# Attention probabilities turned in 32x32 blocks on VectorE and over DRAM instead of on TensorE

## The chip, the cores and the metric

The kernel runs on one core of a Trainium2 chip. The metric is device time in microseconds (us): the median of the runs of one program. A profile is one execution; its span runs from the first to the last instruction. The engines are called by their short names: PE is TensorE (matmuls, and the transposes made with a matmul by the identity), DVE is VectorE, ACT is ScalarE, POOL is GpSimd, and SP is the engine that issues nearly all DMAs.

## The reference

One layer of an encoder over 512 tokens of width 1024, in float32. After an RMSNorm, one projection gives the columns of two branches: attention (8 query heads of 128 in 2 groups, one key and value head each) and a gated delta rule (8 heads, forward and backward). Both are merged through sigmoid gates, projected, added to x after a norm, and a gated per-layer embedding is added. The part that changes is attention:

```
def block(qi):                       # 128 queries at a time
    s = einsum('bkgqd,bksd->bkgqs', qi, k) * scale
    pr = softmax(s, axis=-1)
    return einsum('bkgqs,bksd->bkgqd', pr, v)
...
y_att = (o_att * silu(az)) @ w_br_att
```

`az` is the gate of the attention branch, a projection of the same normed input.

## The kernel before, in words

Every float32 matmul of the large projections is split: each operand is kept as a rounded high part (fp32r) and a low part, and three matmuls (low by high, high by low, high by high) are summed. ACT writes the high part, and DVE or POOL subtracts it to get the low one (`split`). One matmul moves 512 columns; a weight slab (128 output columns, all 1024 inputs) takes 24 of them.

The order of the work is made at build time by a planner (`Flow`). Each piece of the kernel is a Python generator that asks for buffers (`yield "get", tag`), moments (`"at"`), events (`"ev"`) and PE time (`"pe"`); `A`, `V`, `G`, `W` and `Q` put an operation on ACT, DVE, POOL, DVE with POOL kept away, or the DMA queue of SP, each with a length by a table of costs written into the code. The planner runs the generators against these lengths, and the moments that come out fix the order of the instructions on each engine; on the chip each engine works in that order. The text `ORDER` lists the PE jobs: projections (`dk`, `dq`, `dv` of the delta rule, the gates `az`, `dz`, `gA`, `gB`, `kv`, `q0`, `q1`), then the branch projections `ydn` and `yatt`, the output projection `out0`, `out1` and the embedding gate `pg0`, `pg1`. `PR` holds priorities, `OUT0` the places of the four weight blocks of `out0` in the loads, `COOL` and `HOT` the bias between DVE and POOL for a split of data in SBUF, and `SPARE` the large buffers that are lent to the weight stream for a while.

Large buffers are the units `u0` to `u16` (128 partitions of 8 KB). `c2` (four buffers of 128x512), `blk` (three pairs of 128x512), `gi` and `go` (two each, gates in and out), `whi`, `wlo` and `wraw` (two each, weights) and the PSUM banks `mm` (five) and `aux` (three) are the small ones.

Attention before: `q_job` projects four heads at once (`q0`, `q1`), `q_tail` norms and rotates them, and `q_done` starts all eight heads once both halves are ready. In `att_head(h)` PE makes a 128x512 tile of scores for each of four query tiles; DVE takes the row maximum, ACT the exponential with the row sum; DVE inverts the sum and POOL multiplies the tile by it. Then for each of four key tiles PE transposes four 128x128 squares into a bank `mm` by the identity, ACT and DVE split that into `blk`, and three matmuls add to the output `po` (`pv`). The gate `az`, kept in DRAM since its projection, multiplies `po`, and the split result goes to `ya`, the input of `yatt`.

The delta rule already has another way to transpose: `small_blocks` turns each 32x32 block on DVE, and `turned` writes the blocks to DRAM and reads them back to their places.

Of the kernel before, what the change touches and what calls it, by code (L numbers as in the profile page):

```python
# [17 lines left out]
NT = 4  # L18
# [17 lines left out]
class Flow:  # L36
# [73 lines left out]
    def ready(self, want):  # L110
        kind = want[0]
        if kind == "at":
            return want[1]
        if kind == "ev":
            return want[1].t
        s = self.slots[want[1]]
        return min(s) if s else None

# [5 lines left out]
    def run(self):  # L124
        while self.parts:
            best, soon = None, None
            for p in self.parts:
                r = self.ready(p[3])
                if r is None:
                    continue  # L130
                if r <= self.now + 1e-9:
                    if best is None or p[:2] < best[:2]:
                        best = p
                elif soon is None or r < soon:
                    soon = r
            if best is None:
                if soon is None:
                    raise RuntimeError("stuck: " + ", ".join(f"{p[0]} {p[2].__name__} {p[3][:2]}" for p in self.parts))
                self.now = soon
                continue  # L140
            if best[3][0] == "get":
                s = self.slots[best[3][1]]
                s.remove(min(s))
            self.flush()
# [12 lines left out]


ORDER = """
dk0 vec dk1 dq0 dq1 dq3 dq2 dk2 az4 dk3 dv1 dv3 dq5 dv0 dq7 dz7  # L160
dk5 dv2 az3 dz5 dz3 az6 gB2 gB4 dz0 az0 gA3 dk4 dk7 dz4 dq6 dq4
gA4 dk6 gA6 gB5 dz1 dz2 dv7 dv4 dv5 gA0 az1 gA5 gB0 gA2 dv6 az2
gA1 kv gA7 gB7 az7 gB6 gB3 q0 gB1 dz6 q1 az5 free_h ydn0 ydn6 ydn7
ydn5 ydn3 ydn1 ydn2 ydn4 yatt1 yatt0 yatt5 yatt3 yatt7 yatt2 yatt6 yatt4 out0 out1 pg0
# [6 lines left out]
SPARE = ((15, "raw", 7.0, 190.0), (11, "pair", 22.0, 80.0), (12, "pair", 22.0, 80.0), (14, "pair", 279.0, 375.0),  # L171
         (13, "pair", 443.0, 525.0))
EOUT = 24.0
WIDE = 2.0
LAND = "c2"
LONG, NEAR = 0.6, 1.5
X_DVE = ()
WARM = 5.5
W1 = 0
COOL, HOT = 2.5, -1.5  # L180


@with_exitstack
def layer(ctx, tc, x, xT, pw0, wp1, wt, wba, wn, rows, qkn, hd16, npost, pnorm, dnorm, cs, out):
# [261 lines left out]


    slab, blocks, fetched = {}, {}, {}

    lent = {"raw": {}, "pair": {}}  # L450
    held = {}
# [43 lines left out]
    def loader(names):  # L495
        for name in names:
            yield "ev", fetched[name]
            raw, t = load[name]
            if name[:2] in places:
                us, j = places[name[:2]], name[2]  # L500
                his, los = blocks.setdefault(name[1], ([], []))
                if j % 2 == 0:
                    for u, lst in ((us[j // 2], his), (us[j // 2 + 2], los)):
                        yield "get", f"u{u}"
# [979 lines left out]
    def q_job(b, qus):  # L1484
# [5 lines left out]
        o = yield from gemm_k(f"q{b}", hh, hl)  # L1490
        for t in range(NT):
            att_ev[b, t] = spawn(q_tail(b, t, o[t]), PR["q"])
        if b == 1:
            spawn(q_done(), 4)

    def q_done():
        for b in range(2):
            yield "ev", stat_ev["q", b]
            for t in range(NT):
                yield "ev", att_ev[b, t]  # L1500
        free("u16")
        for h in range(8):
            head_ev[h] = spawn(att_head(h), PR["head"] + 0.01 * h)
        att_start.set(F.now)

    head_ev = {}
    att_start = Event()
    ya = [None, None]

    def att_head(h):  # L1510
        hb, kv, b = h % 4, h // 4, h // 4
        qh, ql = qbs[b]
        akT, av = akv["k"], akv["v"]
        if h % 2 == 0:
            yield "get", "u16"
            pu = unit(16, [128, 4, 512])
            P = [pu[:, t, :] for t in range(NT)]
        else:
            P = []
            for t in range(NT):  # L1520
                yield "get", "c2"
                P.append(tile("c2", [128, 512]))
        uz, tz = yield from gate_in("az", h)
        tp = []
        for t in range(NT):
            cc = slice(t * 128, (t + 1) * 128)
            yield "get", "aux"
            sc = bank("aux")
            pe.matmul(sc, ql[:, hb, cc], akT[:, 0, kv, :], start=True, stop=False)  # L1529
# [21 lines left out]
            free("blk", F.now + 0.7)  # L1551

        pend = []
        for kt in range(NT):
            yield "get", "mm"
            pt = bank("mm")
            for t in range(NT):
                pe.transpose(pt[:, t * 128:(t + 1) * 128], P[t][:, kt * 128:(kt + 1) * 128], ident)  # L1558
            yield "pe", 0.436
            yield "get", "blk"  # L1560
            pT = tile("blk", [128, 2, 512], F32R)
            _, tl = split(pt, pT[:, 0], pT[:, 1], F.now, 512)
            free("mm", tl)
            pend.append((kt, pT, tl))
            if len(pend) > 1:
# [4 lines left out]
        if h % 2 == 0:  # L1570
            free("u16")
        else:
            for t in range(NT):
                free("c2")
        k_, p_, t_ = pend.pop(0)
        yield "at", t_ + 0.3
        pv(k_, p_)
        yield "pe", 0.682
# [77 lines left out]
    def yatt_job(n):  # L1656
# [7 lines left out]
        o = yield from gemm_t(("yatt", n), sel(ya, 0), sel(ya, 1), [head_ev[h] for h in range(8)])  # L1664
        att_ev["mix", n] = spawn(yatt_tail(n, o, pre), 5)
        if turn("yatt") == 7:
            for u in (13, 14, 9, 10):
                free(f"u{u}")


# [67 lines left out]
    def out_job(half, us):  # L1738
# [1 line left out]
            yield "get", "u12"  # L1740
            late["mx0"] = unit(12, [128, 4, 512])
        else:
            for u, lst in zip((0, 1, 2, 3), (x1Th, x1Th, x1Tl, x1Tl)):
# [151 lines left out]
    def job(kind, n=0):  # L1895
        if kind in ("dk", "dq", "dv"):
            return conv_job, kind, n
        if kind in GATES:
            return gate_job, kind, n
        return {"kv": (kv_job,), "q": (q_job, n, ((9, 10), (11, 12))[n % 2]), "ydn": (ydn_job, n), "yatt": (yatt_job, n),  # L1900
                "out": (out_job, n, ((0, 1, 2, 3), (6, 15, 16, 11))[n % 2]), "free_h": (call, free_h),
                "vec": (call, late_vectors), "pg": (pg_job, n, ((13, 14, 9, 10), (6, 15, 16, 11))[n % 2])}[kind]
# [93 lines left out]
```

## Time and profile before

| what | value |
|---|---|
| runs | 750.6, 752.1, 752.03 us; median 752.03 |
| span of the profiled execution | 749.9 us |
| what lies around it in the median | 2.1 us |
| PE, DVE, ACT, POOL busy | 98%, 63%, 47%, 42% of the span |
| bytes moved by DMA | 110.99 MB, 148 GB/s in the mean |
| attention on PE (scores to last probability matmul) | 516.3 to 609.9 us (first and last start) |

A row of the profile names the line, the engine, the operation and the tiles it writes and reads (with buffer numbers left out, so `u` is any large unit). Line L122 is the planner's call of an operation, L102 the same for long POOL operations and L97 for those that keep POOL away, so those rows are told apart by their tiles. The profile gives an execution's span and not its whole time; it is set beside the median.

### The profile page before, as it was taken

To read this page: it belongs to the slowest core of one execution; us is meant where nothing else is said; L and a number is where in the kernel's file an instruction comes from. 1 tells how busy PE (TensorE), PEld (TensorE's weight loads), DVE (VectorE), ACT (ScalarE), POOL (GpSimd) and SP (SyncE) were. 2 spreads that over 40 slices of the span, in tenths; PEclk is the share of its full clock that TensorE was granted. 3 is DMA by queue.
4 is the path that set the end of the run, shared out by engine and by line. 5 is a ranking of instruction groups with operands and counts; after the bars stand their busy time and mean duration, and the time that the engine had idled before them with its cause. 6 is when DMAs were issued, how large, how long until landed. Compare 5 with 4: busy or idle time off the path is not lost.

```text
span 749.9 us, 11919 instructions
## 1 busy us (share of the span) xinstructions
PE 736.5 (98%) x4441; PEld 617.5 (82%) x4441; DVE 473.6 (63%) x924; ACT 353.2 (47%) x668; POOL 315.1 (42%) x284
## 2 busy tenths in 40 slices
PE   9999999999899999999999999999999999999996
PEld 7688888888688898888789988888888888888885
DVE  4688989887875657997384535438667744314434
ACT  6659474544552265442633245334576633332422
POOL 5836585213233265300531155657446434561501
PEclk9999999999999999999999999999999999999999
DMA  8854456687402244756521134435233446552323
GB/s 347 299 199 129 162 173 186 197 271 233 116 30 71 76 156 114 229 175 199 138 73 43 43 113 140 154 111 200 87 97 115 137 167 213 176 180 94 99 66 117
DMA packets 65994, 110.99 MB, mean 148 GB/s; under 512 B 22353, under 2 KB 31505, under 8 KB 65937
## 3 DMA queue, kind: packets, MB, share of 16 engines
q1 hardware_dynamic: 65648, 109.98, 45.2%
q8 instruction: 35, 0.57, 0.3%
q10 hardware_dynamic: 288, 0.26, 0.1%
q14 instruction: 23, 0.18, 0.1%
HBM read 87.11 MB, written 23.10 MB: 147 GB/s over the span
## 4 chain that ended last, share of the span: by engine, by line
PE 94%; DMA 2%; ACT 1%; DVE 1%; issue 0%; POOL 0%; POOLq 0%; DVEq 0%
PE mm L534 17%; PE mm L536 17%; PE mm L535 17%; PE mm L555 4%; PE mm L553 4%; PE mm L554 4%; PE mm L571 3%; PE mm L572 3%; PE mm L573 3%; PE aux L1203 2%; PE aux L1235 2%; PE mm L1558 2%; PE aux L1221 2%; PE aux L1194 1%; PE aux L1183 1%; PE aux L1529 1%
## 5 line engine op out<-in xcount | busy, mean ns | idle before, releaser
L102 POOL TENSOR_TENSOR wlo<-wraw,whi 128x1024 fp32r<-128x1024 f32 x52 | 124.3, 2393 | 208.1 <-ACT whi L122 205.4
L534 PE MATMUL mm<-u,wlo 128*128 128x512 f32 x504 | 203.6, 404 | 2.6 <-POOL wlo L102 2.3
L536 PE MATMUL mm<-u,whi 128*128 128x512 f32 x504 | 197.1, 391 | 0.0
L535 PE MATMUL mm<-u,whi 128*128 128x512 f32 x504 | 196.9, 391 | 0.0
L534 PEld LDWEIGHTS mm<-u,wlo 128*128 128x128 f32 x504 | 94.9, 188 | 21.6 <-POOL wlo L102 2.4
L536 PEld LDWEIGHTS mm<-u,whi 128*128 128x128 f32 x504 | 94.7, 188 | 20.3
L535 PEld LDWEIGHTS mm<-u,whi 128*128 128x128 f32 x504 | 95.0, 189 | 17.5 <-DVE u L122 0.3
L122 ACT CAST whi<-wraw 128x1024 fp32r<-128x1024 f32 x63 | 66.0, 1048 | 71.0 <-PE mm L536 40.5
L122 DVE SCALAR_TENSOR_TENSOR f<-mm,cw,f 128x510 f32<-128x510 f32 (+1 forms) x96 | 71.6, 746 | 15.9 <-ACT f L122 13.3
L102 POOL TENSOR_TENSOR u<-wraw,u 128x1024 fp32r<-128x1024 f32 x23 | 55.1, 2401 | 13.7 <-ACT u L122 13.0
L122 DVE TENSOR_TENSOR u<-aux,u 128x512 f32<-128x512 f32 (+2 forms) x60 | 39.4, 670 | 21.2 <-ACT u L122 17.2
L553 PE MATMUL mm<-u,u 128*128 128x512 f32 (+1 forms) x136 | 52.0, 382 | 0.0
L555 PE MATMUL mm<-u,u 128*128 128x512 f32 (+1 forms) x136 | 51.4, 378 | 0.0
L554 PE MATMUL mm<-u,u 128*128 128x512 f32 (+1 forms) x136 | 51.3, 377 | 0.0
L122 ACT CAST u<-aux 128x512 fp32r<-128x512 f32 (+1 forms) x28 | 15.6, 556 | 39.0 <-PE aux L1731 14.1
L122 ACT COPY c<-aux 128x512 f32<-128x512 f32 x18 | 10.6, 586 | 47.6 <-DVE f L122 28.7
L122 ACT ACTIVATE mm<-f 128x512 f32<-128x512 f32 x24 | 14.4, 601 | 38.4 <-DVE f L122 32.6
L571 PE MATMUL mm<-whi,u 128*128 128x512 f32 x80 | 31.6, 395 | 0.0
L572 PE MATMUL mm<-wlo,u 128*128 128x512 f32 x80 | 31.3, 391 | 0.0
L573 PE MATMUL mm<-whi,u 128*128 128x512 f32 x80 | 31.2, 390 | 0.0
L555 PEld LDWEIGHTS mm<-u,u 128*128 128x128 f32 x136 | 25.6, 188 | 4.8
L122 ACT CAST u<-wraw 128x1024 fp32r<-128x1024 f32 x24 | 25.1, 1048 | 9.4 <-DMA wraw<-in_wn_dram 9.4
(261 smaller groups left out, 1453.6 us busy)
## 6 DMA issues: line engine op xcount, KB each, us to landing
wraw<-in_wt_dram SPq DMA_DIRECT2D x59, 512.0 KB, 3.8
wraw<-in_wn_dram SPq DMA_DIRECT2D x28, 512.0 KB, 4.0
u<-in_wt_dram SPq DMA_DIRECT2D x13, 512.0 KB, 5.8
u<-CI SPq DMA_DIRECT2D x16, 256.0 KB, 4.9
u<-in_x_dram SPq DMA_DIRECT2D x4, 512.0 KB, 7.4
u<-in_xT_dram SPq DMA_DIRECT2D x4, 512.0 KB, 8.2
eD<-u SPq DMA_DIRECT2D x8, 256.0 KB, 8.0
Bdk<-f SPq DMA_DIRECT2D x8, 256.0 KB, 2.8
```

Of the source, the lines that this page charges most:

```text
L102: ins = fn(*a, **k)
L122: fn(*a, **k)
L534: pe.matmul(o, lo[:, k, :], mh(k), start=(k == 0), stop=False)
L535: pe.matmul(o, hi[:, k, :], ml(k), start=False, stop=False)
L536: pe.matmul(o, hi[:, k, :], mh(k), start=False, stop=(k == 7))
L553: pe.matmul(o, b, hi, start=(i == 0), stop=False)
L554: pe.matmul(o, a, lo, start=False, stop=False)
L555: pe.matmul(o, a, hi, start=False, stop=(i == 7))
L571: pe.matmul(o[t], b, hi, start=(k == 0), stop=False)
L572: pe.matmul(o[t], a, lo, start=False, stop=False)
L573: pe.matmul(o[t], a, hi, start=False, stop=(k == 7))
L1203: pe.matmul(pw[:, h, :], Vm[g][d][:, 4 * c + h, :], r[:, h, :], start=True, stop=True)
```

## The change

Each head's probabilities stay unnormalised and are transposed without PE. For each of its four query tiles DVE turns the 32x32 blocks of the exponentials (`c2`) into a unit `T` (one of `u13`, `u14`, `u16`, whichever is free), and SP writes them to a DRAM buffer in runs of 512 bytes. When all four are written, four DMAs, one for each quarter of the partitions, read the rows back into another unit `L` in runs of 2 KB, so that `L` holds the transposed probabilities in blocks. ACT and POOL split them from there into `blk`. The inverse row sums go to DRAM (`SR`) as 512 single words, come back as one row spread over all partitions, and POOL multiplies the gate by them. `q_done` now runs for each half: heads 0 to 3 start after `q0`. Buffers move: `ya` to `u0` to `u3`, the weights of `out0` and `x1T` to `u9`, `u13`, `u10`, `u14`; the second half of `out0`'s blocks waits for an event (`landed`) of the last head; the fifth lent unit is gone; and `ORDER`, `OUT0`, `PR` and the biases have new values.

```diff
+            elif best[3][0] == "any":
+                self.got = min((t for t in best[3][1] if self.slots[t]), key=lambda t: min(self.slots[t]))
...
-dk0 vec dk1 dq0 dq1 dq3 dq2 dk2 az4 dk3 dv1 dv3 dq5 dv0 dq7 dz7
+dk1 dk3 dq2 dq0 dq1 dq3 dk2 az2 dk0 dv0 dv3 dk7 dk4 dk6 az5 dv2
...
-OUT0 = 'ydn5 ydn1 ydn4 yatt1'
-PR = dict(dec=8, dm1=8, y=7, conv=9, gate=0, kv=9, q=4, head=6, ple=1, prep=2, tab=1)
+OUT0 = 'yatt4 ydn4 yatt6 yatt7'
+PR = dict(dec=4, dm1=5, y=8, conv=4, gate=5, kv=4, q=9, head=6, ple=9, prep=8, tab=4)
-EXPS = 0.0
...
-         (13, "pair", 443.0, 525.0))
-EOUT = 24.0
+EXPS = 0.41
+EOUT = 30.95
...
-COOL, HOT = 2.5, -1.5
+COOL, HOT = 1.25, -1.24
+HEADU = ("u13", "u14", "u16")
...
+        spawn(q_done(b), 4)
+
+    def q_done(b):
...
+        for h in range(4 * b, 4 * b + 4):
+            head_ev[h] = spawn(att_head(h), PR["head"] + 0.01 * h)
...
-            te = A(0.68, te, act.activation, P[t], sc, AF.Exp, bias=bi, scale=rs, accum_out=li)
+            te = A(0.68, te, act.activation, P, sc, AF.Exp, bias=bi, scale=rs, accum_out=li)
             free("aux", te)
-            te = V(0.15, te, dve.reciprocal, ri, li)
-            tp.append(G(0.72, te, pool.tensor_scalar, out=P[t], in0=P[t], scalar1=ri, scalar2=0.0,
-                        op0=ALU.mult, op1=ALU.add))
-        yield "at", max(tp) + 0.3
+            tr = V(0.15, te, dve.reciprocal, ri, li)
+            te = V(0.64, te, dve.transpose, T[:, :, t].rearrange("p a j q -> p j a q"), P)
+            free("c2", te)
+            tw = Q(2, te, B[:, :, :, t * 128:(t + 1) * 128].rearrange("P i a n -> (P i) a n"),
+                   T[:, :, t].rearrange("p a j q -> p a (j q)"))
+        free(f"u{uT}", tw)
+        tr = Q(1, tr, SR[h].rearrange("(t p) -> p t", p=128), sm[:, :, 3, h])
+        yield "at", tw - 1.0
+        yield "any", HEADU
...
+        for a in range(4):
+            tl = Q(2, tw, L[32 * a:32 * a + 32].rearrange("p P t j q -> p P (t j q)"), B[:, :, a, :].rearrange("P i n -> i P n"))
+        uz, tz = yield from gate_in("az", h)
+        yield "get", "c2"
+        rb = tile("c2", [128, 512])
+        tr = Q(2, tr, rb, row(SR[h], 512))
+        tz = G(1.19, max(tz, tr), pool.tensor_mul, uz, uz, rb)
...
-            for t in range(NT):
-                pe.transpose(pt[:, t * 128:(t + 1) * 128], P[t][:, kt * 128:(kt + 1) * 128], ident)
-            yield "pe", 0.436
...
-            _, tl = split(pt, pT[:, 0], pT[:, 1], F.now, 512)
+                src = L[:, :, :, kt, :].rearrange("p P t q -> p t P q")
+                hi, lo = (pT[:, i].rearrange("p (t P q) -> p t P q", t=4, P=4) for i in range(2))
+                pend.append((kt, pT, split(src, hi, lo, tl, 512, True)[1]))
...
-            us = ((13, 14), (9, 10))[b]
+            us = ((0, 1), (2, 3))[b]
```

Three places show what moves. First PE, in the middle of a head before: `aux_699` is the head's output, L1548 to L1550 are its matmuls with the probabilities, L1558 the transposes and L534 to L536 a weight slab.

```order
L1548 MATMUL aux_699_5150<-blk_701_5157,u15_453_3498 128x512
L1549 MATMUL aux_699_5150<-blk_701_5157,u15_453_3498 128x512
L1550 MATMUL aux_699_5150<-blk_701_5157,u15_453_3498 128x512
L1558 MATMUL mm_707_5193<-ident_65,u16_683_5067 128x128 x4
L1548 MATMUL aux_699_5150<-blk_703_5164,u15_453_3498 128x512
L1549 MATMUL aux_699_5150<-blk_703_5164,u15_453_3498 128x512
L1550 MATMUL aux_699_5150<-blk_703_5164,u15_453_3498 128x512
L1558 MATMUL mm_709_5205<-ident_65,u16_683_5067 128x128 x4
L534 MATMUL mm_712_5214<-u4_363_2836,wlo_678_5022 128x512
L535 MATMUL mm_712_5214<-u5_364_2837,whi_677_5021 128x512
```

The same place of a head (head 4, output `aux_782`, L1571 to L1573) in the changed kernel; L1536 to L1538 make scores of a later head and L543 to L545 are a slab.

```order
L1536 MATMUL aux_797_5613<-u6_449_3499,u12_629_4708 128x512
L1537 MATMUL aux_797_5613<-u6_449_3499,u11_628_4707 128x512
L1538 MATMUL aux_797_5613<-u6_449_3499,u11_628_4707 128x512
L1571 MATMUL aux_782_5565<-blk_783_5566,u15_450_3500 128x512
L1572 MATMUL aux_782_5565<-blk_783_5566,u15_450_3500 128x512
L1573 MATMUL aux_782_5565<-blk_783_5566,u15_450_3500 128x512
L543 MATMUL mm_794_5596<-u4_356_2823,wlo_768_5470 128x512
L544 MATMUL mm_794_5596<-u5_357_2824,whi_767_5469 128x512
L545 MATMUL mm_794_5596<-u4_356_2823,whi_767_5469 128x512
L1571 MATMUL aux_782_5565<-blk_784_5567,u15_450_3500 128x512
L1572 MATMUL aux_782_5565<-blk_784_5567,u15_450_3500 128x512
L1573 MATMUL aux_782_5565<-blk_784_5567,u15_450_3500 128x512
```

The transposes between the matmuls are gone, and `blk_783`, which the first of them reads, now comes from the unit `u16_772` that a DMA has filled. Between head 4's last score matmul and the first of these stand 81 matmuls of other work.

Second the queue of SP in attention before: weights (`wraw`), gates in (`gi`, `go`) and the merged delta branch out (`mixB`).

```order
L122 DMA go_741_5366<-gate_gB_96 128x512
L122 DMA mixB_116<-go_711_5213 128x512
L122 DMA wraw_750_5417<-in_wn_dram 128x1024
L122 DMA gi_765_5495<-gate_az_93 128x512
L122 DMA go_772_5534<-gate_gB_96 128x512
L122 DMA wraw_775_5548<-in_wt_dram 128x1024
L122 DMA mixB_116<-go_741_5366 128x512
L122 DMA wraw_780_5568<-in_wn_dram 128x1024
```

The queue around head 4 in the changed kernel; `P4` is the DRAM buffer of its probabilities, `SR` that of the sums, `u16_772` its unit `L`, and `c2_774` the row sums spread over the partitions.

```order
L124 DMA go_754_5385<-gate_gB_96 128x512
L124 DMA P4_5342<-u16_743_5341 512x1x128
L124 DMA wraw_759_5422<-in_wt_dram 128x1024
L124 DMA SR_116<-sm_104 128x4x1
L124 DMA P4_5342<-u16_743_5341 512x1x128
L124 DMA go_769_5471<-gate_gB_96 128x512
L124 DMA mixB_117<-go_754_5385 128x512
L124 DMA u16_772_5494<-P4_5342 32x4x512
L124 DMA P5_5454<-u13_763_5453 512x1x128
L124 DMA u16_772_5494<-P4_5342 32x4x512 x3
L124 DMA gi_773_5495<-gate_az_93 128x512
L124 DMA c2_774_5496<-SR_116 128x512
```

The last writes and all loads of head 4 stand among the same weights and gates, with a write of head 5 between its first load and the rest, and the row sums come behind the loads.

Third POOL in attention before: normalisations (`u16`, `c2`) between the subtractions of weights.

```order
L102 TENSOR_TENSOR wlo_706_5189<-wraw_681_5054,whi_705_5188 128x1024
L102 TENSOR_TENSOR u2_672_4965<-wraw_694_5100,u0_671_4964 128x1024
L102 TENSOR_SCALAR u16_724_5277<-u16_724_5277,sm_104 128x512 x4
L102 TENSOR_TENSOR wlo_738_5352<-wraw_717_5251,whi_737_5351 128x1024
L102 TENSOR_SCALAR c2_730_5306<-c2_730_5306,sm_104 128x512
L102 TENSOR_SCALAR c2_731_5307<-c2_731_5307,sm_104 128x512
L102 TENSOR_SCALAR c2_732_5308<-c2_732_5308,sm_104 128x512
L102 TENSOR_SCALAR c2_733_5309<-c2_733_5309,sm_104 128x512
L102 TENSOR_TENSOR wlo_762_5492<-wraw_721_5267,whi_761_5491 128x1024
L102 TENSOR_TENSOR u3_764_5494<-wraw_750_5417,u1_763_5493 128x1024
```

POOL in the changed kernel, from head 3's last subtractions (`u14_750`) over head 4's (`u16_772`) to head 5's gate (`gi_800`):

```order
L102 TENSOR_TENSOR wlo_768_5470<-wraw_737_5314,whi_767_5469 128x1024
L102 TENSOR_TENSOR blk_777_5510<-u14_750_5367,blk_777_5510 128x512
L102 TENSOR_TENSOR blk_778_5518<-u14_750_5367,blk_778_5518 128x512
L102 TENSOR_TENSOR gi_773_5495<-gi_773_5495,c2_774_5496 128x512
L102 TENSOR_TENSOR blk_783_5566<-u16_772_5494,blk_783_5566 128x512
L102 TENSOR_TENSOR blk_784_5567<-u16_772_5494,blk_784_5567 128x512
L102 TENSOR_TENSOR wlo_790_5592<-wraw_759_5422,whi_789_5591 128x1024
L102 TENSOR_TENSOR u10_792_5594<-wraw_781_5535,u9_791_5593 128x1024
L102 TENSOR_TENSOR blk_798_5626<-u16_772_5494,blk_798_5626 128x512
L102 TENSOR_TENSOR blk_803_5646<-u16_772_5494,blk_803_5646 128x512
L102 TENSOR_TENSOR gi_800_5628<-gi_800_5628,c2_801_5629 128x512
```

The normalisations are replaced by subtractions from the units into `blk`, and head 4's gate (`gi_773`) is multiplied ahead of its first subtraction (`blk_783`).

More of the change, by code (lines that the diff above doesn't have):

```diff
@@ L115, in ready @@
             return want[1].t
+        if kind == "any":
+            return min((min(self.slots[t]) for t in want[1] if self.slots[t]), default=None)
         s = self.slots[want[1]]
@@ L501, in loader @@
                 his, los = blocks.setdefault(name[1], ([], []))
+                if name[1] == "out0" and j >= 2:
+                    yield "ev", landed
                 if j % 2 == 0:
@@ L1513, in att_head @@
         akT, av = akv["k"], akv["v"]
[L1514 to L1524, printed above, removed]
+        yield "any", HEADU
+        uT = int(F.got[1:])
+        T = unit(uT, [128, 4, 4, 4, 32])
+        B = dram(f"P{h}", [4, 32, 4, 512])
         for t in range(NT):
             cc = slice(t * 128, (t + 1) * 128)
+            yield "get", "c2"
+            P = tile("c2", [128, 512])
             yield "get", "aux"
@@ L1569, in att_head @@
                 yield "pe", 0.682
[L1570 to L1578, printed above, removed]
+        free(f"u{uL}", t_)
+        if turn("landed") == 7:
+            landed.set(F.now)
         if ya[b] is None:
-            us = ((13, 14), (9, 10))[b]
+            us = ((0, 1), (2, 3))[b]
             ya[b] = "pending"
@@ L1666, in yatt_job @@
         if turn("yatt") == 7:
-            for u in (13, 14, 9, 10):
+            for u in (0, 1, 2, 3):
                 free(f"u{u}")
@@ L1742, in out_job @@
         else:
-            for u, lst in zip((0, 1, 2, 3), (x1Th, x1Th, x1Tl, x1Tl)):
+            for u, lst in zip((9, 13, 10, 14), (x1Th, x1Th, x1Tl, x1Tl)):
                 yield "get", f"u{u}"
```

55 lines of the change are left out of this document (30 added, 25 removed).

## The prediction

> **What bounds the kernel now.** I read the head of the page first, then what TensorE (PE) waited for.
>
> ```profile
> span 749.9 us, 11919 instructions
> PE 736.5 (98%) x4441; PEld 617.5 (82%) x4441; DVE 473.6 (63%) x924; ACT 353.2 (47%) x668; POOL 315.1 (42%) x284
> PE 94%; DMA 2%; ACT 1%; DVE 1%; issue 0%; POOL 0%; POOLq 0%; DVEq 0%
> PE mm L534 <- POOL wlo L102: 2.3, 1, 2.3
> PE mm L1859 <- POOL ident masks.py:199: 1.4, 1, 1.4
> 0.00:25.00 25.00, 22.56 (x99) 17.86 (x100) 14.95 (x23) 17.36 (x30) 14.16 (x40) 1.00 0.89 329
> 720.00:749.90 29.90, 22.45 (x122) 19.40 (x120) 13.03 (x22) 6.58 (x18) 3.70 (x10) 0.96 0.26 88
> ```
>
> PE is busy 98% of the span and carries 94% of the chain that ended last; its longest wait is 2.3 us. The last two rows are stretches (from:to, length, then PE busy): of the 13.4 us that PE is idle 2.4 lie in the first 25 us and 7.4 after the last matmul. So an instruction taken off PE shortens the kernel by its time, as long as nothing makes PE wait instead. Does the "busy" PE run at full pace where the transposes stand? The timeline of PE near the end of attention:
>
> ```profile
> 597.30 0.39 PE L1549 MATMUL aux<-blk,u 128*128 128x512 f32 x1
> 597.53 0.39 PE L1550 MATMUL aux<-blk,u 128*128 128x512 f32 x1
> 597.76 0.60 PE L1558 MATMUL mm<-ident,u 128*128 128x128 f32 x4
> 598.12 0.48 PE L1548 MATMUL aux<-blk,u 128*128 128x512 f32 x1
> 598.43 0.40 PE L1549 MATMUL aux<-blk,u 128*128 128x512 f32 x1
> ```
>
> The first column is the start. A matmul of 512 columns follows the one before after 0.23 us, without gaps. Four transposes delay the next matmul by 0.36 us, and the matmul behind them takes 0.31 instead of 0.23: 0.44 us per four.
>
> **The change: what leaves PE.**
>
> ```profile
> L1558 PE MATMUL mm<-ident,c 128*128 128x128 f32 x64 | 9.3, 272 | 0.0
> L1558 PE MATMUL mm<-ident,u 128*128 128x128 f32 x64 | 8.9, 272 | 0.0
> ```
>
> 128 transposes in 32 fours, all gone from the new order: 32 x 0.44 = 14.1 us. The other PE work is the same in number. With no new wait the span is 749.9 - 14.1 = 735.8.
>
> **What the other engines get.** Rows of the old attention (some as min/median/max ns, then the first and last start), and the nearest rows for the new operations:
>
> ```profile
> L122 DVE TENSOR_REDUCE sm<-aux x32: 673/681/692, 517.2 to 597.0; 128x1 f32<-128x512 f32 x32
> L122 DVE TENSOR_SCALAR sm<-sm,saq x32: 196/214/216, 518.0 to 597.7; 128x1 f32<-128x1 f32 x32
> L122 ACT ACTIVATE u<-aux,sm,saq x16: 777/779/799, 518.3 to 590.3; 128x512 f32<-128x512 f32 x16
> L122 ACT ACTIVATION_READ_ACCUMULATOR u<-aux,sm,saq x16: 187/191/216, 518.9 to 591.0; 128x1 f32 x16
> L122 DVE TENSOR_TENSOR blk<-mm,blk 128x512 fp32r<-128x512 f32 x32 | 21.5, 685 | 8.3 <-ACT blk L122 8.0
> L122 DVE STREAM_TRANSPOSE f<-f 128x512 f32<-128x512 f32 x8 | 5.6, 700 | 0.0
> L102 POOL TENSOR_SCALAR u<-u,sm 128x512 f32<-128x512 f32 x16 | 11.1, 694 | 21.4 <-DVE sm L122 10.7 <-PE aux L1550 10.7
> L102 POOL TENSOR_TENSOR u<-u,u 128x512 fp32r<-128x512 f32 x4 | 5.2, 1297 | 6.0 <-DVE wlo L97 4.4 <-DVE u L97 0.7 <-ACT u L122 0.7
> L122 ACT CAST whi<-wraw 128x1024 fp32r<-128x1024 f32 x63 | 66.0, 1048 | 71.0 <-PE mm L536 40.5 <-PE mm L573 14.1 <-DMA wraw<-in_wn_dram 6.1
> L102 POOL TENSOR_TENSOR wlo<-wraw,whi 128x1024 fp32r<-128x1024 f32 x52 | 124.3, 2393 | 208.1 <-ACT whi L122 205.4 <-ACT u L122 1.1 <-DVE u L968 0.9
> ```
>
> DVE loses the 32 subtractions blk<-mm,blk (0.685) and gains 32 block transposes (0.70): +0.5 us. POOL loses 32 normalisations (0.69, 22 us) and gains 32 subtractions (1.30) and 8 gate multiplications (taken as 1.30 too): 52 us, net +30. Per head POOL then has 5 x 1.3 plus one weight subtraction (2.4) = 8.9 us, where PE spends about 11 us: 80%, so no bound by itself. ACT's exponential and casts stay. These cost PE nothing unless they are late in a chain.
>
> **The new chain of a head.** Between the last score matmul of heads 4, 5 and 6 and their first matmul with the probabilities, the new PE order has 81 matmuls: 81 x 0.228 = 18.4 us of cover. Heads 2 and 3 have 18 and 20, head 7 has 69 matmuls, 15.7 us; heads 0 and 1 have 22 and 27. What must fit into it: reduce 0.68, exponential 0.78 with its small neighbours 0.21 and 0.19, transpose 0.70 (2.6 together), then DMA:
>
> ```profile
> Bdv<-f SPq DMA_DIRECT2D x8, 256.0 KB, 2.2
> gi<-gate_az SPq DMA_DIRECT2D x8, 256.0 KB, 3.3
> c<-Bdv SPq DMA_DIRECT2D x32, 64.0 KB, 2.3
> L122 SPq DMA_DIRECT2D c<-Bdv x32: 302/430/1437, 92.9 to 354.4; - x32
> ```
>
> The write lands after 2.2 us (same shape of packets as the Bdv writes). Then SP issues four loads, the gate and the row sums, 6 x 0.43 = 2.6, and the last lands 3.3 later. In POOL's order the gate multiplication stands ahead of the head's first subtraction, so the subtraction waits for the row sums' two transfers as well: 1.3 + 1.3. With some ten handoffs of about 0.15 (an estimate from the first starts above: 517.2 + 0.68 to 518.0, 518.0 + 0.21 to 518.3) the chain is 2.6 + 2.2 + 5.9 + 2.6 + 1.5 = 14.8 us, under 18.4.
>
> That holds on a quiet queue. From the first write of head 2 to the last load of head 7 the new SP order has 71 transfers of 256 KB (24 writes, 24 loads, 23 of gates, sums and mixes), 8 of 512 KB and 6 of row sums (512 words of 4 bytes): 71 x 0.262 + 8 x 0.524 = 22.8 MB, while PE has about 305 matmuls to do, 70 us. That asks for 326 GB/s. What the trace shows (the last two columns are the DMA engines' busy share and GB/s):
>
> ```profile
> 108.00:110.00 2.00, 2.00 (x15) 1.80 (x14) 1.72 (x3) 2.00 (x7) 2.00 (x4) 1.00 0.92 352
> 128.00:130.00 2.00, 2.00 (x10) 1.66 (x9) 1.89 (x4) 1.64 (x2) 0.83 (x1) 1.00 1.02 297
> 150.00:160.00 10.00, 10.00 (x46) 8.27 (x45) 8.10 (x16) 6.38 (x16) 1.27 (x2) 1.00 0.93 325
> 500.00:610.00 110.00, 110.00 (x553) 90.28 (x552) 78.67 (x175) 63.87 (x123) 59.74 (x58) 1.00 0.39 129
> 620.00:720.00 100.00, 100.00 (x458) 82.72 (x457) 33.82 (x50) 34.29 (x56) 45.11 (x32) 1.00 0.44 146
> ```
>
> Attention now runs the DMA at 0.39; the new one would need what 150:160 shows, 0.93, for 70 us on end. At 352 GB/s the 22.8 MB take 65 us (no loss), at 297 they take 77 (loss 7, without any pause). And landings grow under load; in 140 to 172 us, where the share is 78%:
>
> ```profile
> q1 hardware_dynamic: 4479, 8.42, 78.2%
> E<-u SPq DMA_DIRECT2D x4, 256.0 KB, 4.7
> gate_dz<-go SPq DMA_DIRECT2D x3, 256.0 KB, 7.1
> gate_gB<-go SPq DMA_DIRECT2D x2, 256.0 KB, 4.5
> ```
>
> A write takes 2.3 to 4.9 us longer than the quiet 2.2, a load up to 1.4 longer than 3.3 (taking E<-u). The chain becomes 17 to 21 us: from 1.4 under to 2.7 over the cover of heads 2 to 6, and 1.4 to 5.4 over that of head 7. Loss by latency: 0 + 1.4 at the least, 5 x 2.7 + 5.4 = 19 at the most; the middle (0.6 x 5 + 3.4) is 6.4. A wait for one head is cover for the next, which makes the upper end generous. I take 6, near the middle and within the 0 to 7 of the throughput; both ends stay for the range. Sum: 749.9 - 14.1 + 6 = 741.8.
>
> The Trainium skill, SBUF — State Buffer, section on the DMA port swizzle, says that a transfer into 32 partitions reaches eight of the sixteen ports and measured 189 GB/s there against 328 with all, and that two such transfers serialize. No run here shows a large load of that kind; by its figures 24 loads would take 33 us instead of 19 (an estimate), and the sum would be about 14 us higher.
>
> **Edits with one answer.** Two weight pairs instead of a third lent one: a slab needs cast and subtraction, about 1.05 + 2.4, under its 24 x 0.228 = 5.5 us on PE, and 620:720 shows PE busy 100.00 of 100 with two; if POOL were late, up to 2.4 per slab. The late row vectors are needed by the first tail of out0, while its other tiles hold PE for 22 us and a fifth bank is free: nothing. New homes and the wait for the last head in front of half of out0's blocks: eight yatt slabs (44 us) lie between: nothing. The new order of projections shifts waits of which the old order has some 6 us in all: -2 to +6, taken as 0.
>
> The runs shown have a median of 752.03, 2.1 above this execution's span; with that, 741.8 gives 744.
>
> **The rivals.** (1) Hidden: if the landings stay quiet, the 14.8 us chain fits everywhere and the gain is whole: 735.8 to 738 of span, 738 to 740 in time. For it: the first landings of each head are written early, one block at a time, so only the last write is in the chain. Against it: 0.93 asked of the DMA.
> (2) The loads into a quarter of the partitions are the new bound, and it ends slower. Place: the four loads of each head. Price: at half of 326 GB/s a 256 KB load takes 1.6 us instead of 0.8, 24 x 0.8 = 19 us more in a stretch without slack: 749.9 - 14.1 + 19 = 755, in time 757. It decides from a loss of 14.1, 0.6 us per load. Against it: c<-Bdv loads of the same partitions land in 2.3 us, though they are a quarter as large. The page of the Trainium skill named above speaks for it.
> (3) The new order of projections opens waits elsewhere, of 5 to 20 us: 741 to 756 of span, 743 to 758 in time. For it: every engine's order changes from the first row. Against it: old waits of 6 us in all under the same rules.
> That the transposes don't leave is excluded by the order; that they lay in PE's own slack is against the pace of 0.23.
>
> **How the numbers follow.** Forecast (loss 2 to 11, time 740 to 749): 0.44. Hidden: 0.26. Loads as the bound (loss 11 to 25, 749 to 763): 0.20. Elsewhere: 0.10. Two tenths of a per cent, 1.5 us, is about what a measurement tells from no change. Faster: 0.44 + 0.26 + 0.02 of each of the last two = 0.74; same 0.11 (0.08 of the loads, 0.03 of elsewhere); slower 0.15. The range 736 to 757 leaves out about 0.05 below, since a start-up wait may go too, and 0.10 above.
>
> **What would show it.** Right: no transposes by identity in attention; PE waits of 4 to 10 us in all on L1571 for POOL's blk; DMA share above 0.8 there; landings of the probability writes of 3 us or more and of the loads of 4 to 6. The hidden case: PE waits as short as now. The load case: loads that land after 7 us or more. What would make me wrong most: POOL, through the gate multiplication ahead of the subtractions, or waits ahead of attention.

## The result: 9.6% slower, and the profile after

| kernel | median of the runs | span of the profile | ratio to before (95% interval) |
|---|---|---|---|
| before | 752.07 us | 749.9 us | 1 |
| changed | 823.55 us | 821.2 us | 1.0956 (1.0929 to 1.0983) |

The forecast was 744, in a range of 736 to 757. The head of the changed kernel's page (busy time, share of the span and instructions of each engine, and the chain that ended last):

```profile
span 821.2 us, 11817 instructions
PE 746.9 (91%) x4313; PEld 615.3 (75%) x4313; DVE 475.9 (58%) x926; ACT 354.2 (43%) x672; POOL 336.9 (41%) x289
PE 60%; DMA 21%; POOL 6%; DVE 5%; ACT 3%; issue 2%; SPq 2%; POOLq 0%; DVEq 0%; ACTq 0%
```

What PE waited for longest in it (its tile and line, who released it, then the sum of the waits in us, their count and the longest):

```profile
PE aux L1571 <- ACT blk L124: 17.9, 4, 7.2
PE aux L1572 <- POOL blk L102: 14.9, 5, 5.7
PE aux L1536 <- DVE u L124: 13.3, 2, 10.7
PE aux L1571 <- ACT c L124: 6.5, 1, 6.5
PE aux L1536 <- ACT c L124: 5.4, 2, 4.0
```

PE executes 128 instructions fewer, yet it is busy 10 us longer and idle 821.2 - 746.9 = 74 us where it was idle 13. It waits for the casts and subtractions of the probabilities (L1571, L1572). At a head's scores (L1536) it waits for a PSUM bank `aux`. Where the longest of these waits comes from stands in the timelines of ACT, DVE and PE (the bracket has the idle time before the instruction in us and what ended it):

```profile
607.99 0.62 ACT L124 CAST blk<-u 128x512 fp32r<-128x512 f32 x1 [13.71 <-DMA u<-P]
609.13 0.69 DVE L124 TENSOR_TENSOR u<-aux,u 128x512 fp32r<-128x512 f32 x1 [11.92 <-ACT u L124]
609.88 0.80 PE L1536 MATMUL aux<-u,u 128*128 128x512 f32 x1 [10.65 <-DVE u L124]
```

ACT waits 13.7 us for the loads of a head's probabilities. Its cast of an earlier head's output stands behind that in its order, DVE's subtraction waits for this cast, and only then is the bank free for the next scores. So late loads hold up PE in two places. 21% of the chain that ended last is now DMA, where it was 2%. The stretches by stage (PE busy, then at the end the granted clock, the DMA share and GB/s):

```profile
0.00:480.00 480.00, 473.62 (x3173) 397.40 (x3174) 346.40 (x680) 240.24 (x467) 192.38 (x178) 1.00 0.48 155
480.00:660.00 180.00, 127.95 (x481) 98.45 (x480) 75.85 (x167) 63.18 (x118) 76.40 (x58) 0.83 0.85 167
660.00:821.20 161.20, 145.30 (x661) 119.48 (x659) 53.64 (x81) 50.81 (x87) 68.08 (x53) 0.95 0.47 157
```

The loss is made in attention, 480 to 660 us: 52 of the 74 idle us, and a granted clock of 0.83. The DMA engines are busy 85% of that time and still move only 167 GB/s; in the kernel before, 0.93 went with 325. Something occupies them without moving bytes. The same view in windows of 2 us, while an early head's probabilities were on their way:

```profile
486.00:488.00 2.00, 2.00 (x11) 1.65 (x10) 1.93 (x5) 0.61 (x1) 0.00 (x0) 1.00 2.11 71
488.00:490.00 2.00, 2.00 (x11) 1.65 (x10) 1.69 (x5) 2.00 (x5) 0.00 (x0) 1.00 0.65 7
490.00:492.00 2.00, 2.00 (x10) 1.67 (x9) 0.00 (x0) 0.05 (x1) 1.87 (x1) 1.00 1.10 17
492.00:494.00 2.00, 2.00 (x10) 1.66 (x9) 0.00 (x0) 0.00 (x0) 0.52 (x1) 1.00 0.95 34
```

And the timeline of SP's queue shortly before (start, duration, tiles):

```profile
482.75 0.58 SPq L124 DMA_DIRECT2D SR<-sm  x1
483.42 2.74 SPq L124 DMA_DIRECT2D P<-u  x2
486.26 0.58 SPq L124 DMA_DIRECT2D wraw<-in_wt_dram  x1
```

A share of 1.2 in the mean of the four (in windows so short a share can pass 1) at 7 to 71 GB/s, right behind the issue of `SR<-sm`, the 512 inverse row sums that are written as single words of 4 bytes. The DMA groups of the whole changed kernel (count, size, median us to landing):

```profile
P<-u SPq DMA_DIRECT2D x32, 256.0 KB, 7.7
u<-P SPq DMA_DIRECT2D x32, 256.0 KB, 6.3
SR<-sm SPq DMA_DIRECT2D x8, 2.0 KB, 12.7
```

2 KB take 12.7 us to land, and the writes of probabilities beside them 7.7 where like writes took 2.2 before. The same view of two short windows separates the writes of probabilities by their place in the queue: first the three that SP issued just ahead of the first `SR<-sm` (478 to 482.5 us), then the three right behind it (483 to 487 us).

```profile
P<-u SPq DMA_DIRECT2D x3, 256.0 KB, 2.7
P<-u SPq DMA_DIRECT2D x3, 256.0 KB, 11.1
```

Ahead of the single words such a write lands in 2.7 us, behind them in 11.1.

### The profile page after: what moved, and what is told of

The parts are those of the page before. It is cut to its first block, busy times and chain, and to the rows that moved or that the text cites. A ratio compares the mean times of both kernels' runs of the same rounds, so it can differ in the third digit from the quotient of the medians.

```text
span 821.2 us, 11817 instructions
## 1 busy us (share of the span) xinstructions
PE 746.9 (91%) x4313; PEld 615.3 (75%) x4313; DVE 475.9 (58%) x926; ACT 354.2 (43%) x672; POOL 336.9 (41%) x289
## 4 chain that ended last, share of the span: by engine, by line
PE 60%; DMA 21%; POOL 6%; DVE 5%; ACT 3%; issue 2%; SPq 2%; POOLq 0%; DVEq 0%; ACTq 0%
PE mm L543 10%; PE mm L545 10%; PE mm L544 10%; DMA P<-u 9%; DMA u<-P 4%; PE mm L564 3%; PE mm L562 3%; PE mm L563 3%; POOL wlo L102 3%; SPq L124 2%; PE aux L1212 2%; DMA go<-gate_gB 2%; PE aux L1244 2%; DMA c<-SR 2%; PE mm L581 2%
## 5 line engine op out<-in xcount | busy, mean ns | idle before, releaser
L543 PE MATMUL mm<-u,wlo 128*128 128x512 f32 x520 | 212.3, 408 | 5.0 <-POOL wlo L102 2.5
L544 PE MATMUL mm<-u,whi 128*128 128x512 f32 x520 | 205.9, 396 | 0.0
L545 PE MATMUL mm<-u,whi 128*128 128x512 f32 x520 | 205.8, 396 | 0.0
L543 PEld LDWEIGHTS mm<-u,wlo 128*128 128x128 f32 x520 | 99.9, 192 | 28.8 <-POOL wlo L102 4.4
L545 PEld LDWEIGHTS mm<-u,whi 128*128 128x128 f32 x520 | 99.5, 191 | 21.7
L544 PEld LDWEIGHTS mm<-u,whi 128*128 128x128 f32 x520 | 99.7, 192 | 18.9
L124 DVE SCALAR_TENSOR_TENSOR f<-mm,cw,f 128x510 f32<-128x510 f32 (+1 forms) x96 | 71.5, 746 | 14.4 <-ACT f L124 12.0
L102 POOL TENSOR_TENSOR u<-wraw,u 128x1024 fp32r<-128x1024 f32 x19 | 45.5, 2401 | 17.7 <-ACT u L124 17.7
L124 ACT CAST blk<-u 128x512 fp32r<-128x512 f32 x32 | 19.2, 617 | 76.4 <-DMA u<-P 65.3
L102 POOL TENSOR_TENSOR gi<-gi,c 128x512 f32<-128x512 f32 x8 | 10.2, 1270 | 93.6 <-DMA c<-SR 47.9
L102 POOL TENSOR_TENSOR blk<-u,blk 128x512 fp32r<-128x512 f32 x32 | 41.2, 1310 | 0.2
L1571 PE MATMUL aux<-blk,u 128*128 128x512 f32 x32 | 16.1, 504 | 24.4 <-ACT blk L124 17.9
L124 ACT ACTIVATE c<-aux,sm,saq 128x512 f32<-128x512 f32 x32 | 24.9, 778 | 30.6 <-DVE sm L124 30.3
L97 DVE TENSOR_TENSOR wlo<-wraw,whi 128x1024 fp32r<-128x1024 f32 x13 | 16.0, 1231 | 35.5 <-ACT whi L124 35.5
L580 PE MATMUL mm<-whi,u 128*128 128x512 f32 x88 | 34.7, 395 | 0.0
```

What stands on the lines that cost most here:

```text
L102: ins = fn(*a, **k)
L124: fn(*a, **k)
L543: pe.matmul(o, lo[:, k, :], mh(k), start=(k == 0), stop=False)
L544: pe.matmul(o, hi[:, k, :], ml(k), start=False, stop=False)
L545: pe.matmul(o, hi[:, k, :], mh(k), start=False, stop=(k == 7))
L580: pe.matmul(o[t], b, hi, start=(k == 0), stop=False)
```

## The experiments

Two theories stood at the start. Theory 1: the single words of the row sums hold the DMA engines, and all that is queued behind them is late. Theory 2, my rival: the bytes of the probabilities, and loads into a quarter of the partitions, are the bound. Where an order of instructions is said to be the same, only the named DMA differs; sr16, the kernels that build on it, srpad and srpad64 also have one more transfer at the start, which fills `SR` with a constant. Ratios are to the kernel before.

**sr16: 16 words instead of 512.**

```diff
-        tr = Q(1, tr, SR[h].rearrange("(t p) -> p t", p=128), sm[:, :, 3, h])
+        tr = Q(1, tr, SR[h, 0:16].rearrange("(t p) -> p t", p=4), sm[0:4, :, 3, h])
```

> The changed kernel in the same order on every engine, but each head writes 16 inverse row sums to DRAM (four partitions, four words each) instead of 512; the other 496 stay at a constant, so the gate is scaled by wrong numbers. Theory 1 (the 512 single words of 4 bytes hold all DMA engines for some 8 us per head, and everything behind them waits): the DMA share in attention falls under 0.8, PE's waits fall from 66 us to under 15, and the time to 738 to 752. Theory 2 (the 16 MB of probabilities and the loads into a quarter of the partitions are the bound, as in my rival): the 2 KB taken away change nothing, time 800 to 823.

Measured 773.76 us, 1.0295 (1.0269 to 1.0321): 50 us of the 71.5 are gone, with 2 KB less per head. Theory 1 has the larger part. It does not have all, and the time lies in neither of my ranges: PE's waits still sum to some 28 us, and the DMA share in attention is 0.81 (its row stands below). What the remaining 22 us are is asked further down.

**srpt, srpad, srpad64: where the words lie.** The 512 words again, in other places of DRAM: in srpt each partition's four words side by side in one piece of 16 bytes, in srpad every word 512 bytes from the next, in srpad64 64 bytes. The edit of srpt:

```diff
+        tr = Q(1, tr, SR[h].rearrange("(p t) -> p t", t=4), sm[:, :, 3, h])
```

and in srpad, where srpad64 has 16 for 128 in the first line:

```diff
+    SW = dram("SW", [8, 512, 128])
+        tr = Q(1, tr, SW[h, :, 0].rearrange("(t p) -> p t", p=128), sm[:, :, 3, h])
```

> The changed kernel in the same order, but the four sums of a partition lie side by side in DRAM, so that the write has 128 pieces of 16 bytes instead of 512 of 4 (the row read back has the sums in another order, so the gate is scaled by wrong numbers). Theory 1a (a price per piece): the write takes a quarter, some 2 us, and the time falls to 745 to 765. Theory 1b (pieces of different partitions in one stretch of DRAM hold each other up): nearly as slow as before, 800 to 823. Theory 2: 815 to 823.

> The changed kernel in the same order, but the 512 words are written 512 bytes apart into a buffer that nobody reads; the row read back is a constant, so the gate is not scaled and the row's load does not wait for the write. Theory 1a (a price per piece): the writes hold the DMA as long as before, time 800 to 823. Theory 1b (pieces in one stretch of DRAM hold each other up): the write falls to 1 or 2 us and the time to 740 to 765. Theory 2: 815 to 823.

> As the kernel whose words go 512 bytes apart, but 64 bytes apart. If words hold each other up that lie in one 64-byte line: near 770. If in one stretch of 512 bytes: 800 to 823.

Measured: srpt 829.86 us, 1.1032 (1.0966 to 1.1099), no better with a quarter of the pieces and above my range for that, 800 to 823; srpad 770.61, 1.0245 (1.0202 to 1.0287), above its range of 740 to 765; srpad64 768.0, 1.0203 (1.0182 to 1.0223), near the 770 that I gave. In that loaded queue the words land after 5.9 and 6.3 us, not the 1 or 2 that I expected of srpad. 512 words that lie 64 bytes apart cost no more than 16 words, and 128 pieces of 16 bytes side by side cost as much as 512 words side by side. So it is not the number of pieces; it is how close together they lie. Two things change together here, though: with words 64 bytes apart the whole row takes 32 KB of DRAM instead of 2 KB. Whether neighbours within 64 bytes matter, or so many pieces in one stretch of 2 KB, these runs do not separate. In srpad and srpad64 the row that is read back also no longer waits for the write, so their gain is not that of the distance alone.

**bsr and bsr64: the words alone, in the kernel before.** Written behind each head's scores, read by nobody; side by side in bsr:

```diff
+        Q(1, te, SR[h].rearrange("(t p) -> p t", p=128), sm[:, :, 3, h])
```

and 64 bytes apart in bsr64:

```diff
+        Q(1, te, SW[h, :, 0].rearrange("(t p) -> p t", p=128), sm[:, :, 3, h])
```

> The kernel before with one thing added: behind each head's scores the 512 inverse sums of that head are written to DRAM as single words, and nobody reads them. Theory 1: each write holds the DMA engines for some 8 us, the weights and gates queued behind land that much later, and PE waits for some of them: 755 to 800. Theory 2 (these writes cost next to nothing): 750 to 753.

> The kernel before with 512 inverse sums of each head written to a DRAM buffer that nobody reads, the words 64 bytes apart. If the price lies in words that share a 64-byte line: landings of 3 us or less where the neighbouring words took 13, and 751 to 754 instead of 760. If it is a price per word: 757 to 762.

Measured: bsr 759.73 us, 1.01 (1.0057 to 1.0143); bsr64 752.09, 0.9999 (0.9987 to 1.0011). The DMA group of the words in bsr, then its attention in the view by windows:

```profile
SR<-sm SPq DMA_DIRECT2D x8, 2.0 KB, 13.1
```

```profile
500.00:640.00 140.00, 136.71 (x660) 111.31 (x659) 88.58 (x189) 71.33 (x133) 70.54 (x63) 0.99 0.59 138
```

The same two of bsr64:

```profile
SW<-sm SPq DMA_DIRECT2D x8, 2.0 KB, 2.2
```

```profile
500.00:640.00 140.00, 140.00 (x684) 114.95 (x683) 90.40 (x192) 72.61 (x134) 72.65 (x64) 1.00 0.47 146
```

13.1 against 2.2 us to landing, with nothing but the distance of the words (and so the stretch that they fill) changed. The Trainium skill, DMA: Bandwidth & Descriptors, says in its specifications that transfers below 512 bytes do read-modify-write. That alone is not the price here: the words of bsr64 are as short and land in 2.2 us; only side by side do they cost. The DMA share falls by 0.12 of 140 us, 17 us of all sixteen engines for eight writes: 2 us each, not the some 8 of theory 1. In this kernel, whose attention uses the DMA at 0.47 with the words apart (bsr64), the words cost 7 us (two runs, 4 to 11 by the interval); in the changed one, where a head waits for the transfers behind them, 50.

**neworder: the new tables alone.** The functions of before with the new `ORDER`, `OUT0`, `PR`, biases and lent units.

```diff
-dk0 vec dk1 dq0 dq1 dq3 dq2 dk2 az4 dk3 dv1 dv3 dq5 dv0 dq7 dz7
+dk1 dk3 dq2 dq0 dq1 dq3 dk2 az2 dk0 dv0 dv3 dk7 dk4 dk6 az5 dv2
```

> The kernel before, its transposes on TensorE, with the new order of jobs, priorities, biases and lent buffers alone. If the new order is harmless (theory 1 and 2, the loss is made in the new transposes' DMAs): 747 to 757. If it opens waits elsewhere (rival 3): 757 to 772.

Measured 755.72 us, 1.0046 (1.0031 to 1.006): 3.3 us slower, within "harmless", but not nothing. My rival of waits elsewhere is worth 3 us, under the 5 to 20 that I gave it.

**full128, wq, wlq: what is left with 16 words.** All three build on sr16 and keep the order. full128 loads each block into all partitions (so that what `L` holds is not in the reference's order). It also reads one stretch of 256 KB in DRAM, where the loads before took runs of 2 KB, 8 KB apart:

```diff
-            tl = Q(2, tw, L[32 * a:32 * a + 32].rearrange("p P t j q -> p P (t j q)"), B[:, :, a, :].rearrange("P i n -> i P n"))
+            tl = Q(2, tw, L[:, a].rearrange("p t j q -> p (t j q)"), B[a].rearrange("i a n -> (i a) n"))
```

wq writes a quarter, so that the loads read block 0 alone:

```diff
+            tw = Q(2, te, B[:, :, 0, t * 128:(t + 1) * 128].rearrange("P i n -> (P i) n"),
+                   T[:, 0, t].rearrange("p j q -> p (j q)"))
```

wlq is wq with a quarter of each load too:

```diff
+            tl = Q(2, tw, L[32 * a:32 * a + 32, 0].rearrange("p t j q -> p (t j q)"), B[0, :, 0, :])
```

> The kernel with 16 words of sums, but each of the four loads fills all 128 partitions with one run of 2 KB instead of 32 partitions with four (the same bytes and packets; the rows land in a wrong order, so the keys do not fit the values). If the quarter of the partitions was what made the loads slow (rival 2): loads land 2 us earlier or more, and the time falls from 774 to 745 to 760. If it is the volume: 768 to 778.

> The kernel with 16 words of sums, each write of probabilities cut to a quarter (64 KB, the first of four blocks of keys); the loads keep their size and all read that block. If the volume is what is left of the loss: 3 MB per 4 heads less, the DMA share falls from 1.0 to about 0.8 and the time to 748 to 760. If it is the chain of dependent steps, not the volume: 765 to 775.

> As the one with quarter writes, and each load cut to a quarter too (32 partitions with one run of 2 KB; the casts and subtractions read that run four times). The steps, their order and their waits stay, the probabilities' bytes fall to a quarter. If the volume is what is left: DMA share in attention about 0.6, PE waits under 12 us in all, 738 to 748. If the steps or the new order are: above 758.

Measured: full128 764.9 us, 1.0161 (1.0124 to 1.0198); wq 769.8, 1.0226 (1.0188 to 1.0264); wlq 746.2, 0.9913 (0.9882 to 0.9943). The group of a head's loads among the DMA issues of sr16, and its attention in the view by windows:

```profile
u<-P SPq DMA_DIRECT2D x32, 256.0 KB, 5.7
```

```profile
480.00:640.00 160.00, 141.46 (x580) 110.86 (x580) 86.16 (x184) 73.05 (x134) 90.46 (x67) 0.95 0.81 227
```

The same two of full128:

```profile
u<-P SPq DMA_DIRECT2D x32, 256.0 KB, 3.9
```

```profile
480.00:640.00 160.00, 148.04 (x622) 117.28 (x621) 88.98 (x187) 75.89 (x137) 97.35 (x69) 0.97 0.76 238
```

Of wq:

```profile
u<-P SPq DMA_DIRECT2D x32, 256.0 KB, 5.0
```

```profile
480.00:640.00 160.00, 146.08 (x609) 114.66 (x608) 88.57 (x188) 74.48 (x135) 91.56 (x68) 0.97 0.68 193
```

And of wlq:

```profile
u<-P SPq DMA_DIRECT2D x32, 64.0 KB, 2.5
```

```profile
480.00:640.00 160.00, 156.15 (x689) 126.71 (x688) 94.08 (x196) 81.45 (x144) 106.36 (x73) 1.00 0.59 184
```

The same bytes into all 128 partitions land 1.8 us earlier and move faster (238 against 227 GB/s at a lower share): 9 us of time, between my two ranges. Whether the partitions or the one stretch in DRAM does it was not separated. Writing a quarter of the bytes saves 4 us, which missed the 748 to 760 that I gave the volume; loading a quarter too saves 24 more. With the steps and their order all in place and a quarter of the bytes, the change gains 6 us on before. So the steps by themselves are not the bound.

Is it the volume, then, or how late the loads land? The share of the DMA alone does not order the times: wq has the lower share (0.68 against full128's 0.76) and the longer time (769.8 against 764.9). The landing of the loads does: 5.7 us in sr16, 5.0 in wq, 3.9 in full128 and 2.5 in wlq go with 773.8, 769.8, 764.9 and 746.2. srpad64 stands beside the row by some 3 us (5.6 and 768.0), with a row of sums that doesn't wait. This fits a head that waits for its loads before PE can go on, but it is read from few kernels: wlq changed bytes and landings at once, and full128 the way of the loads along with their landings.

**fix8, mix4, mix2: the change without the words and the quarter loads.** POOL normalises the exponentials as before, so no sums travel; the blocks are taken from every fourth column, so that each load is one 256 KB stretch in all partitions and in the right order. `DMAH` names the heads that go over DRAM; the others are transposed on PE.

```diff
+            te = G(0.72, te, pool.tensor_scalar, out=P, in0=P, scalar1=ri, scalar2=0.0, op0=ALU.mult, op1=ALU.add)
...
+                te = V(0.7, te, dve.transpose, T[:, :, t].rearrange("p a j q -> p j a q"),
+                       P.rearrange("p (j i a) -> p j a i", j=4, a=4))
...
+                tl = Q(LKB, tw, L[:, a].rearrange("p t j q -> p (t j q)"), B[a].rearrange("i a n -> (i a) n"))
```

> The changed kernel made right another way, all eight heads over DRAM: POOL normalises the probabilities as in the kernel before, so that no sums go to DRAM and no gate is scaled; the 32x32 blocks are taken from every fourth column, so that each load is 256 KB in one stretch into all 128 partitions. If the words of the sums cost 50 us and the quarter loads 9, and the row of sums 1 MB each: 752 to 766, the volume's share of the loss is left. If the parts are not additive: above 770.

> As fix8, but only heads 0, 2, 4 and 6 go over DRAM and the others are transposed on TensorE as before: 7 us of PE saved, half the bytes; the planner counts 0.95 us for such a transfer. If the volume in the attention is what is left: DMA share there about 0.65, waits near those of the new order alone, 748 to 753. If the steps of the chain are: 755 to 762.

> As mix4, with heads 0 and 1 alone over DRAM, which start early, beside q1: 3.5 us of PE saved. By the volume: 750 to 754, near the new order alone (755.7) less 3.5.

Measured: fix8 762.46 us, 1.0126 (1.011 to 1.0142); mix4 755.33, 1.0042 (1.0027 to 1.0057); mix2 753.19, 1.0013 (1.0003 to 1.0023). Mending the sums and the loads takes off 61 of the 71 us, and keeping more heads on PE brings the time nearer to before. (A head's row of sums is a load of 256 KB, not the 1 MB of my expectation.) mix4 missed the range of the volume (748 to 753) and lies at the low end of the one that I gave the steps of the chain (755 to 762), though its DMA share from 480 to 640 us is 0.56.

**mix2o and mix4o: the same with the old order.** The jobs, priorities and biases of before; in mix4o `DMAH` is heads 0, 2, 4 and 6.

```diff
-OUT0 = 'ydn5 ydn1 ydn4 yatt1'
+OUT0 = 'ydn4 yatt5 yatt6 yatt4'
+DMAH = (0, 1)
```

> As mix2 (heads 0 and 1 over DRAM, the rest on TensorE, POOL normalises), with the jobs, priorities and biases of the kernel before. If the new order's 3.3 us are what mix2 lacks: 748 to 751. If the volume or the chain of the two heads costs the 3.5 us that PE saves: 752 to 755.

> As mix4 (heads 0, 2, 4 and 6 over DRAM), with the jobs, priorities and biases of the kernel before. If four heads' bytes fit between the others and the order was the rest: 746 to 751. If they do not fit even spread: 753 to 760.

Measured: mix2o 753.21 us, 1.0016 (1.0004 to 1.0029); mix4o 761.18, 1.012 (1.0102 to 1.0137). The old order is no better, and with four heads it is worse by 6 us, above both ranges that I gave, so the 3.3 us of the new order are not what the mixed kernels lack. In none of the versions that compute the layer do the transfers of two, four or eight heads cost less than the PE time they save; no version here beats before.

## Why the prediction was wrong

- **What leaves PE.** Right: no transposes of probabilities by the identity are left. wlq shows the size: PE is busy 723.8 us there, 12.7 less than before, near the 14.1 of the sum. The engines' row of wlq's page:

```profile
PE 723.8 (97%) x4313; PEld 602.8 (81%) x4313; DVE 475.5 (64%) x926; ACT 354.1 (48%) x672; POOL 335.4 (45%) x289
```

- **The chain of a head: this is the step that failed.** It put the write at 2.2 us quiet and 4.5 to 7.1 loaded, and counted the row sums as "6 of row sums (512 words of 4 bytes)" among the transfers, with 2 KB and hence no time. That term was put at 0 where the write took 12.7 us of landing per head, and it stands in the same queue as the probabilities, the gates and the weights: writes of probabilities behind it landed after 11.1 us instead of 2.7. sr16 and srpad64 put its part at 50 to 56 us of the 71.5 (50 with 16 words, 56 with words 64 bytes apart, where the row of sums also no longer waits for the write). No row of the old trace had such a write; I should have bounded it from both sides instead of counting its bytes.
- **"A wait for one head is cover for the next"** did not hold either. The heads share the banks `aux` and the order of ACT, so a head whose loads were late kept the next head's scores waiting (the 13.71, 11.92 and 10.65 us above).
- **The loss by throughput and latency, taken as 6.** Too small as well. sr16 is 36 us above the 738 that the sum gave without a loss. Of these 3.3 are the new order (neworder), 9 the way of the loads (full128) and 24 the loaded and 4 the written bytes (wlq, wq; parts overlap, so they are not a sum). The direction was right (a demand of 326 GB/s in attention), but I took the ends of the chain's landings from a stretch at 78% of the old trace, and I did not count what idleness does to PE's clock.
- **The signs.** Most of those named for "right" came true without the forecast: the DMA share in attention was 0.85, writes landed after 7.7 us (3 or more) and loads after 6.3 (4 to 6, nearly). Only PE's waits, 66 us instead of 4 to 10, told the cases apart. What I had named as most likely to make me wrong showed as well, in POOL's waits (sum, count and longest in us):

```profile
POOL gi L102 <- DMA c<-SR: 47.9, 5, 14.0
```

The gate multiplications waited for the row of sums, ahead of the subtractions for which PE waited 14.9 us. In sr16 PE still waits 11.3 us for those; no run moved the gate multiplication behind them; fix8 has no row of sums at all, but differs in more than that.
- **PE's clock was in no term.** Two long waits of PE in the changed kernel, with one matmul between them, in PE's timeline:

```profile
508.61 0.79 PE L1571 MATMUL aux<-blk,u 128*128 128x512 f32 x1 [7.18 <-ACT blk L124]
515.07 0.79 PE L1572 MATMUL aux<-blk,u 128*128 128x512 f32 x1 [5.67 <-POOL blk L102]
```

The windows around it (PE busy first, the granted clock third from the end):

```profile
502.00:504.00 2.00, 0.00 (x0) 0.00 (x0) 0.00 (x0) 0.00 (x0) 0.00 (x0) 1.00 1.58 230
504.00:506.00 2.00, 0.00 (x0) 0.00 (x0) 0.00 (x0) 0.00 (x0) 0.00 (x0) 0.72 1.37 54
506.00:508.00 2.00, 0.00 (x0) 0.00 (x0) 0.00 (x0) 0.07 (x1) 0.00 (x0) 0.50 0.80 58
508.00:510.00 2.00, 0.79 (x1) 0.29 (x1) 0.00 (x0) 1.07 (x2) 0.00 (x0) 0.50 1.09 199
510.00:512.00 2.00, 0.00 (x0) 0.00 (x0) 0.00 (x0) 0.00 (x0) 0.00 (x0) 0.50 0.61 193
512.00:514.00 2.00, 0.00 (x0) 0.00 (x0) 0.00 (x0) 0.32 (x1) 1.48 (x2) 0.50 0.70 166
514.00:516.00 2.00, 0.94 (x2) 0.83 (x3) 1.24 (x1) 2.00 (x4) 2.00 (x2) 0.50 1.09 240
516.00:518.00 2.00, 2.00 (x6) 1.53 (x5) 1.97 (x5) 1.22 (x3) 1.23 (x1) 0.50 1.07 211
518.00:520.00 2.00, 2.00 (x9) 1.60 (x9) 2.00 (x5) 0.62 (x1) 0.00 (x0) 0.86 1.05 332
520.00:522.00 2.00, 2.00 (x12) 1.68 (x11) 1.97 (x5) 0.03 (x1) 1.29 (x1) 1.00 0.97 383
```

The first wait begins at 501.4. The granted clock is at 1.00 up to 504 and halved from about 505 on (0.72 in the mean of 504 to 506), some 3.5 us into the wait. The single matmul at 508.61 does not bring it back. Steady work begins again at 515.07, and the clock is full again from about 518.6 (0.86 in the mean of 518 to 520), some 3.5 us later; until then one matmul follows another after 0.43 us instead of 0.23. PE is busy 746.9 us with the same 4313 matmuls and transposes that take 723.8 in wlq, where the clock in attention is 1.00: some 23 us of slower matmuls on top of the waits. The Trainium skill, TensorE: Matmul & The Clock Gate, in the section Why this matters for your kernels, warns of gaps over about 3 us between matmuls; this trace agrees, with the clock falling some 3.5 us into the wait.
- **Rival 2** had a right place, the four loads of each head, and the right sign, but not the price: 9 us, not 19, measured where the words no longer held up the queue. The Trainium skill, SBUF — State Buffer, section on the DMA port swizzle, which I had weighed for it, gave 14 by its figures (an estimate); full128 goes the same way, but it changes the reading of DRAM too, so it does not show the ports as the cause.
- **POOL** and **DVE** were no bound by their sums: 41% and 58% of the span, where they were 42% and 63% before.

## What to carry to other kernels

Price a small DMA by where its pieces land, not by its bytes: 512 words from 128 partitions into one 2 KB row took 13 us to land and held up what was queued behind, and one word per 64 bytes cost the kernel before nothing that could be measured. The DMA, off the bound at a share of 39%, became a bound when work was moved onto it: sum the new bytes against the stage in which they fall, and price a dependent chain with the landings of a stage as loaded as the new one. A wait of over some 3.5 us on PE costs its length and then the slow clock behind it.

## What the runs showed of the hardware

- 512 words of 4 bytes from 128 partitions, side by side in 2 KB of DRAM, land in 13.1 us (bsr), against 2.2 us with one word per 64 bytes (bsr64). In the changed kernel 128 pieces of 16 bytes side by side (srpt) are no better than the 512 words: 14.5 us against 12.7. Distances between 16 and 64 bytes were not tried, nor fewer words further apart in one stretch of 2 KB, nor what holds the writes up.
- Loads of 256 KB into 32 partitions, from runs of 2 KB, land in 5.7 us where 128 partitions, from one stretch, take 3.9, in the same order of instructions (sr16, full128).
- PE's granted clock fell to half some 3.5 us into a wait and was full again some 3.5 us after steady work began (the changed kernel, 501 to 520 us).
